# Prompt self-attention: each head group's score and value matmuls as one chained piece

## The chip, the cores and the metric

The kernel runs on one core of a Trainium2 chip. The metric is device time in microseconds from the start to the end of one execution; the median of the runs counts. PE is TensorE, DVE is VectorE, ACT is ScalarE, POOL is GpSimd, SP is SyncE, which issues the transfers. An instruction is named by the line of the kernel that made it, so L875 is line 875 of the kernel before; a line can be that of a helper.

## What is computed

One inference step of a two-layer decoder with 256 prompt tokens and 32 new tokens of eight sequences (288 columns in all). Each layer does, in short:

```python
proj = x @ w_in                                   # q, k, v of 12 heads of 64, and u, gate
q, k = rope_partial(q), rope_partial(k)
for g, (window, dilation) in enumerate(((128, 1), (512, 4), (2048, 16))):   # 4 heads each
    s = q . k[rows at distance 0, d, 2d .. window] / 8
    o[g], lse[g] = softmax(s) @ v, m + log(sum(exp(s - m)))
att = softmax(lse, over g) * o
sgu = u * (tril(w_spatial) @ layer_norm(gate) + b_spatial)
x = layer_norm(alpha * x + concat(att, sgu) @ w_mix_out)
x = layer_norm(alpha * x + cross_attention(x, memory) @ w_xo)
x = layer_norm(alpha * x + relu(x @ w_up) ** 2 @ w_down)
```

The prompt attends to itself; each new token attends to the cached keys and values of its own sequence (three caches a layer) and to the new rows.

## The kernel before

Activations lie with channels on the partitions and the 288 tokens in the free direction. A projection (`linear`, `mm3`) goes over output tiles of 128 channels; each tile is 8 input chunks with three matmuls each (L361 wh x H, L362 wh x L, L363 wl x H), since weights and activations are split into a high and a low part. ACT makes the high part wh of a weight tile (L343), DVE the low part wl (L344).

Attention is done beside the projections. A planner (`Tasks`) holds background generators with a priority; `tasks.run` draws from them as the main projection goes on, and `tasks.drain` empties them. After that a scheduler puts the instructions of each engine in their final order by priority and readiness; what stands inside `tc.high_priority()` is taken ahead of others. A dependency of kind NoSync fixes the order of two instructions on one engine without a semaphore. `burst` (L308) uses both: all its matmuls are urgent and chained. Before, only the cross-attention of the new tokens calls it.

The parts that the change and the prediction touch:

- `prompt_scores(p)` (L864), for p = 0 and 1 and three groups g: two heads (h2 = 0 and 1) in the upper and lower 64 partitions. Each head has a 256-wide score matmul (L875) and a 128-wide one (L879), f32, into a tile `tr` of its own. DVE adds the mask and takes the maximum (L883), then the softmax (L889 to L902); three transposes a group and head (L906, L908) turn the probabilities into `pt`.
- `prompt_pv(p)` (L916): for each g a 256-wide (L925) and a 128-wide (L928) value matmul for each of the two heads into one tile `acc`, which ACT and DVE copy out to attH and attL.
- `decode_scores` (L949): scores of the new tokens against the caches. GpSimd and DVE multiply cache tiles `cu` by the query (L1034 on DVE), DVE reduces them (L1035) and spreads the sums into `zs` (L1041); PE's L1047 turns zs into scores. L974 scores the new keys.
- `decode_pv` (L1090): L1101 multiplies cache value tiles `cu` with the probabilities `z`, four matmuls for each cache tile; o_1287 and o_1288 are two accumulators of layer 0, and the four tiles of o_1288 are the last ones. L1111 adds the new rows, L1122 transposes the result.
- `rope` writes the rotated q and k (L699, GpSimd among others); L777, L793 and L1014 transpose them and the values. `sgu` has L845 and L850.
- `cu` tiles are five buffers of one stream, loaded by SP in a fixed order (L148); a transfer is issued when a buffer is released by its last reader.
- The output projection starts with L361 on attH.

PSUM has three pools: `acc` with 3 tiles, `tr` with 3, `dec` with 2.

Of the kernel before, what the change touches and what calls it, by code (L numbers as in the profile page):

```python
# [1 line left out]

# [1 line left out]

# [224 lines left out]
def build(ctx, tc, I, O, worder, corder, recording):  # L229
    nc = tc.nc  # L230
    V, S, G, T = nc.vector, nc.scalar, nc.gpsimd, nc.tensor
# [23 lines left out]
    def acc(name="acc"):  # L255
        return pp.tile([128, 512], F32, name=name, tag="acc", bufs=3)
# [48 lines left out]
            tc.add_manual_dep(ins.ins, gates[name].ins.name, dep, reason="behind")  # L305
        return ins

    def burst(calls):  # L308

        last = None  # L310
        with tc.high_priority():
            for out, lhsT, rhs, start, stop in calls:
                m = T.matmul(out, lhsT, rhs, start=start, stop=stop, skip_group_check=True)
                if last is not None and not recording:
                    dep = mybir.DependencyInfo(mybir.DependencyClass.NoSync, mybir.DependencyReason.DATA)
                    tc.add_manual_dep(m.ins, last.ins.name, dep, reason="burst")
                last = m

    class Weights:
        pos = 0  # L320
# [383 lines left out]
    def layer(l, xH, xL, norm):  # L704
        tasks.flags.clear()
        flag = tasks.flag
        qT = slot([128, 6, TOK], name="qT")
        kT = slot([128, 6, TOK], name="kT")
        vn = slot([128, 2304], name="vn")
# [154 lines left out]
        def prompt_scores(p):  # L864
            pt = slot([128, 2, 3, 384], name="pt")
# [4 lines left out]
                ms.append(small(12, "m"))  # L870
            for g in range(3):
                b = [tr(), tr()]
                for h2 in range(2):
                    r = slice(64 * h2, 64 * h2 + 64)
                    T.matmul(b[h2][:, 0:256], qT[r, 2 * g + p, 128:256], kT[r, 2 * g + p, 0:256],  # L875
                             start=True, stop=True)
                for h2 in range(2):
                    r = slice(64 * h2, 64 * h2 + 64)
                    T.matmul(b[h2][:, 256:384], qT[r, 2 * g + p, 0:128], kT[r, 2 * g + p, 0:128],  # L879
                             start=True, stop=True)  # L880
                for h2 in range(2):
                    for i, (k0, k1, c) in enumerate(((0, 256, 0), (256, 384, 128))):
                        V.tensor_tensor_reduce(out=sc[h2][:, g, k0:k1], in0=b[h2][:, k0:k1], in1=mq[:, g, c:256],  # L883
                                               scale=1.0, scalar=-3e38, op0=ALU.add, op1=ALU.max,
                                               accum_out=ms[h2][:, 3 * i + g:3 * i + g + 1])
                yield 700, 1500
# [29 lines left out]
        def prompt_pv(p):  # L916
            H, L, pt = att["H"], att["L"], att.pop(f"pt{p}")
            for g in range(3):
                ps = acc()
                for tt in range(2):  # L920
                    for h2 in range(2):
                        c = 256 * g + 64 * (2 * p + h2)
                        o = ps[64 * h2:64 * h2 + 64]
                        if tt == 0:
                            T.matmul(o[:, 0:256], vn[:, c:c + 64], pt[:, h2, g, 0:256],  # L925
                                     start=True, stop=False, skip_group_check=True)
                        else:
                            T.matmul(o[:, 128:256], vn[:, 768 + c:768 + c + 64], pt[:, h2, g, 256:384],  # L928
                                     start=False, stop=True, skip_group_check=True)
                S.activation(H[:, 2 * g + p, 0:256], ps[:, 0:256], AF.Copy)  # L930
                V.tensor_sub(L[:, 2 * g + p, 0:256], ps[:, 0:256], H[:, 2 * g + p, 0:256].bitcast(F32))
                yield 650, 0
# [547 lines left out]
```

## Time and profile before

| | |
|---|---|
| median of 3 runs | 1077.78 us (1076.4 to 1078.43) |
| profiled execution | 1072.3 us |
| its span | 1070.6 us, mean granted TensorE clock 0.982 |
| PE busy | 1025.8 us, 96% of the span, 8038 matmul records |
| DVE busy | 769.4 us, 72% |
| ACT busy | 531.7 us, 50% |
| POOL busy | 191.4 us, 18% |

How to read it: PE is nearly always busy, so the stretches are to be looked at where it isn't. The trace's ends of matmuls are modelled; the distance from one start to the next says more of a matmul's cost than its length. An f32 matmul shows as two records, a pair of records on each half of the array for the two heads. In the profile, "[2.20 <-POOL kT L699]" behind an instruction means that its engine was idle for 2.20 us before it and that POOL's write of kT ended that. The granted clock is 1.00 at 2.4 GHz and 0.50 at 1.2 GHz.

### The profile page before, as it was taken

How to read it: one execution, taken by the hardware profiler on the slowest of the kernel's cores; microseconds unless marked ns; L12 is line 12 of the kernel's file. 1: busy time of each engine (PE TensorE's matmuls, PEld its weight loads, DVE VectorE, ACT ScalarE, POOL GpSimd, SP SyncE). 2: the span in 40 equal slices, each digit the busy share in tenths (PEclk: the TensorE clock that was granted, in tenths of full speed). 3: DMA queues.
4: the chain of work that ended last, by engine and by line, in shares of the span. 5: the costliest groups of instructions: out<-in, count | busy, mean ns of one | idle time of the engine just before them, and what ended most of it. 6: DMA issues, size and time to landing. Idle time of an engine off the chain costs nothing. (4 is left out here: it accounts for less than half of the span.)

```text
span 1070.6 us, 20130 instructions
## 1 busy us (share of the span) xinstructions
PE 1025.8 (96%) x8038; PEld 958.1 (89%) x8038; DVE 769.4 (72%) x1406; ACT 531.7 (50%) x1000; POOL 191.4 (18%) x151
## 2 busy tenths in 40 slices
PE   8999999999999999999978999999999999999995
PEld 7989689988799999999967995998888999999994
DVE  6698679855489756565998987897464996565656
ACT  4437546543458535353553374565353685354431
POOL 4593013000033000000458500220000410000000
PEclk8999999999999999999989899999999999999997
DMA  9989844777944555544436898357874465546431
GB/s 281 303 255 323 230 184 149 250 262 257 328 131 142 191 168 181 158 158 160 155 123 204 240 304 257 119 167 233 289 278 159 136 178 169 182 162 193 166 115 44
DMA packets 185533, 213.68 MB, mean 200 GB/s; under 512 B 5760, under 2 KB 175136, under 8 KB 185440
## 3 DMA queue, kind: packets, MB, share of 16 engines
q1 hardware_dynamic: 177216, 205.00, 60.1%
q10 hardware_dynamic: 8224, 7.41, 2.1%
q8 instruction: 63, 1.03, 0.4%
q14 instruction: 30, 0.25, 0.1%
HBM read 203.80 MB, written 8.59 MB: 198 GB/s over the span
## 5 line engine op out<-in xcount | busy, mean ns | idle before, releaser
L343 ACT ACTIVATE wh<-wraw 128x1024 fp32r<-128x1024 f32 (+1 forms) x237 | 249.5, 1054 | 297.1 <-PE acc L362 237.5
L344 DVE TENSOR_TENSOR wl<-wraw,wh 128x1024 fp32r<-128x1024 f32 (+1 forms) x237 | 311.0, 1315 | 100.4 <-ACT wh L343 99.4
L361 PE MATMUL acc<-xH,wh 128*128 128x288 f32 x728 | 219.4, 302 | 6.7 <-DVE fy L527 4.8
L363 PE MATMUL acc<-xH,wl 128*128 128x288 f32 x728 | 218.4, 301 | 3.1 <-DVE wl L344 3.1
L362 PE MATMUL acc<-xL,wh 128*128 128x288 f32 x728 | 219.0, 301 | 0.0
L361 PE MATMUL acc<-hH,wh 128*128 128x288 f32 x512 | 151.3, 295 | 0.0
L363 PE MATMUL acc<-hH,wl 128*128 128x288 f32 x512 | 151.0, 295 | 0.0
L362 PE MATMUL acc<-hL,wh 128*128 128x288 f32 x512 | 151.0, 295 | 0.0
L361 PEld LDWEIGHTS acc<-xH,wh 128*128 128x128 f32 x728 | 139.7, 192 | 8.0 <-issue 5.0
L363 PEld LDWEIGHTS acc<-xH,wl 128*128 128x128 f32 x728 | 139.2, 191 | 4.7 <-DVE wl L344 4.2
L362 PEld LDWEIGHTS acc<-xL,wh 128*128 128x128 f32 x728 | 139.6, 192 | 1.0 <-DVE fy L751 0.4
L545 POOL TENSOR_TENSOR s<-s,xres 128x288 f32<-128x288 f32 x15 | 20.3, 1354 | 445.8 <-DVE s L541 445.2
L362 PEld LDWEIGHTS acc<-hL,wh 128*128 128x128 f32 x512 | 96.4, 188 | 0.0
L361 PEld LDWEIGHTS acc<-hH,wh 128*128 128x128 f32 x512 | 96.3, 188 | 0.0
L363 PEld LDWEIGHTS acc<-hH,wl 128*128 128x128 f32 x512 | 96.2, 188 | 0.0
L361 PE MATMUL acc<-fH,wh 128*128 128x290 f32 x256 | 78.2, 306 | 1.9 <-DVE fy L527 1.9
L362 PE MATMUL acc<-fL,wh 128*128 128x290 f32 x256 | 76.8, 300 | 0.0
L363 PE MATMUL acc<-fH,wl 128*128 128x290 f32 x256 | 75.8, 299 | 0.6 <-DVE wl L344 0.6
L361 PEld LDWEIGHTS acc<-fH,wh 128*128 128x128 f32 x256 | 48.4, 189 | 2.6 <-PE acc L363 2.3
L362 PEld LDWEIGHTS acc<-fL,wh 128*128 128x128 f32 x256 | 48.5, 190 | 0.8 <-DVE fL L519 0.2
L363 PEld LDWEIGHTS acc<-fH,wl 128*128 128x128 f32 x256 | 48.0, 189 | 1.2 <-DVE wl L344 1.1
L1032 POOL TENSOR_TENSOR cu<-cu,qb 128x1024 f32<-128x1024 f32 x15 | 43.0, 2886 | 9.9 <-DMA qb<-qd 9.5
(320 smaller groups left out, 2184.5 us busy)
## 6 DMA issues: line engine op xcount, KB each, us to landing
cu<-cache_mem_kv SPq DMA_DIRECT2D x64, 512.0 KB, 7.2
wraw<-w_up SPq DMA_DIRECT2D x32, 1024.0 KB, 5.5
wraw<-w_down SPq DMA_DIRECT2D x32, 1024.0 KB, 4.8
wraw<-w_in SPq DMA_DIRECT2D x21, 1024.0 KB, 6.5
cu<-cache_kv_w SPq DMA_DIRECT2D x42, 512.0 KB, 7.2
wraw<-w_xkv SPq DMA_DIRECT2D x16, 1024.0 KB, 6.3
wraw<-w_mix_out SPq DMA_DIRECT2D x8, 1024.0 KB, 10.3
wraw<-w_xq SPq DMA_DIRECT2D x8, 1024.0 KB, 4.8
```

What stands on the lines that cost most here:

```text
L343: S.activation(h[:, r], raw[:, r], AF.Copy)
L344: gates[f"split{k}"] = behind(V.tensor_sub(lo[:, r], raw[:, r], h[:, r].bitcast(F32)), "dve")
L361: m = T.matmul(ps, wh[:, k], H[:, k], start=first, stop=False)
L362: T.matmul(ps, wh[:, k], L[:, k], start=False, stop=False)
L363: T.matmul(ps, wl[:, k], H[:, k], start=False, stop=last)
L545: eng.tensor_add(self.s, self.s, xres[:, n])
L1032: G.tensor_mul(cu, cu, qb[g])
```

## The change

`burst` gets a second argument. With `urgent=False` its first matmul keeps its ordinary priority; the others are urgent and chained behind it as before. `prompt_scores` and `prompt_pv` now collect the four matmuls of a group and queue them with `burst(calls, False)`: first both heads' 256-wide matmuls (h2 = 1, then 0), then both 128-wide ones. Before, none of these was urgent or chained, and h2 = 0 came first. No matmul, copy or transfer is added or taken away, and every operand is the same. In the kernel after, these matmuls carry line L313 (in `burst`), and lines behind `prompt_scores` move up by one (L906 is L905).

```diff
--- before.py
+++ after.py
@@ -1,4 +1,4 @@
-from contextlib import ExitStack
+from contextlib import ExitStack, nullcontext
 
 import numpy as np
 
@@ -305,16 +305,16 @@
             tc.add_manual_dep(ins.ins, gates[name].ins.name, dep, reason="behind")
         return ins
 
-    def burst(calls):
+    def burst(calls, urgent=True):
 
         last = None
-        with tc.high_priority():
-            for out, lhsT, rhs, start, stop in calls:
+        for out, lhsT, rhs, start, stop in calls:
+            with tc.high_priority() if last is not None or urgent else nullcontext():
                 m = T.matmul(out, lhsT, rhs, start=start, stop=stop, skip_group_check=True)
-                if last is not None and not recording:
-                    dep = mybir.DependencyInfo(mybir.DependencyClass.NoSync, mybir.DependencyReason.DATA)
-                    tc.add_manual_dep(m.ins, last.ins.name, dep, reason="burst")
-                last = m
+            if last is not None and not recording:
+                dep = mybir.DependencyInfo(mybir.DependencyClass.NoSync, mybir.DependencyReason.DATA)
+                tc.add_manual_dep(m.ins, last.ins.name, dep, reason="burst")
+            last = m
 
     class Weights:
         pos = 0
@@ -870,14 +870,13 @@
                 ms.append(small(12, "m"))
             for g in range(3):
                 b = [tr(), tr()]
-                for h2 in range(2):
-                    r = slice(64 * h2, 64 * h2 + 64)
-                    T.matmul(b[h2][:, 0:256], qT[r, 2 * g + p, 128:256], kT[r, 2 * g + p, 0:256],
-                             start=True, stop=True)
-                for h2 in range(2):
-                    r = slice(64 * h2, 64 * h2 + 64)
-                    T.matmul(b[h2][:, 256:384], qT[r, 2 * g + p, 0:128], kT[r, 2 * g + p, 0:128],
-                             start=True, stop=True)
+                calls = []
+                for q, c, d in (((128, 256), (0, 256), (0, 256)), ((0, 128), (0, 128), (256, 384))):
+                    for h2 in (1, 0):
+                        r = slice(64 * h2, 64 * h2 + 64)
+                        calls.append((b[h2][:, d[0]:d[1]], qT[r, 2 * g + p, q[0]:q[1]], kT[r, 2 * g + p, c[0]:c[1]],
+                                      True, True))
+                burst(calls, False)
                 for h2 in range(2):
                     for i, (k0, k1, c) in enumerate(((0, 256, 0), (256, 384, 128))):
                         V.tensor_tensor_reduce(out=sc[h2][:, g, k0:k1], in0=b[h2][:, k0:k1], in1=mq[:, g, c:256],
@@ -917,16 +916,17 @@
             H, L, pt = att["H"], att["L"], att.pop(f"pt{p}")
             for g in range(3):
                 ps = acc()
+                calls = []
                 for tt in range(2):
-                    for h2 in range(2):
+                    for h2 in (1, 0):
                         c = 256 * g + 64 * (2 * p + h2)
                         o = ps[64 * h2:64 * h2 + 64]
                         if tt == 0:
-                            T.matmul(o[:, 0:256], vn[:, c:c + 64], pt[:, h2, g, 0:256],
-                                     start=True, stop=False, skip_group_check=True)
+                            calls.append((o[:, 0:256], vn[:, c:c + 64], pt[:, h2, g, 0:256], True, False))
                         else:
-                            T.matmul(o[:, 128:256], vn[:, 768 + c:768 + c + 64], pt[:, h2, g, 256:384],
-                                     start=False, stop=True, skip_group_check=True)
+                            calls.append((o[:, 128:256], vn[:, 768 + c:768 + c + 64], pt[:, h2, g, 256:384],
+                                          False, True))
+                burst(calls, False)
                 S.activation(H[:, 2 * g + p, 0:256], ps[:, 0:256], AF.Copy)
                 V.tensor_sub(L[:, 2 * g + p, 0:256], ps[:, 0:256], H[:, 2 * g + p, 0:256].bitcast(F32))
                 yield 650, 0
```

Two places in PE's order, in which the scheduler put the work differently. In these rows "x2" stands for two matmuls alike, and a name in brackets is the engine or queue whose semaphore is waited for.

PE at the end of attention of layer 0, before: o_1288 takes the last four cache tiles (z, L1101), tr takes probability transposes (p, L906 and L908), acc takes value products (pt, L925).

```order
L1101 MATMUL o_1288<-cu,z_90 32x256 [waits DMAHW1_49,DMAHW0_49]
L906 MATMUL tr<-const,p_1210 128x128 [waits Activation_49]
L908 MATMUL tr<-const,p_1210 128x128 x2
L906 MATMUL tr<-const,p_1210 128x128 [waits Activation_49]
L908 MATMUL tr<-const,p_1210 128x128 x2
L1101 MATMUL o_1288<-cu,z_90 32x256 x3
L1101 MATMUL o_1288<-cu,z_90 32x256 [waits DMAHW3_49,DMAHW2_49]
L1101 MATMUL o_1288<-cu,z_90 32x256 x3
L1111 MATMUL o_1287<-vn,pn 128x256 x2
L925 MATMUL acc<-pt,vn 64x256 [waits Activation_49]
L925 MATMUL acc<-pt,vn 64x256 [waits DVE_49,Activation_49]
L1101 MATMUL o_1288<-cu,z_90 32x256 [waits DMAHW5_49,DMAHW4_49]
```

The same place after:

```order
L1101 MATMUL o_1288<-cu,z_90 32x256 [waits DMAHW1_49,DMAHW0_49]
L1101 MATMUL o_1288<-cu,z_90 32x256 x3
L817 MATMUL tr<-const,misc 32x128 [waits DVE_49]
L817 MATMUL tr<-const,misc 32x128
L1101 MATMUL o_1288<-cu,z_90 32x256 [waits DMAHW3_49,DMAHW2_49]
L1101 MATMUL o_1288<-cu,z_90 32x256 x3
L1101 MATMUL o_1288<-cu,z_90 32x256 [waits DMAHW5_49,DMAHW4_49]
L1101 MATMUL o_1288<-cu,z_90 32x256 x3
L1101 MATMUL o_1288<-cu,z_90 32x256 [waits DMAHW7_49,DMAHW6_49]
L1101 MATMUL o_1288<-cu,z_90 32x256 x3
L1111 MATMUL o_1288<-vn,pn 128x256
L905 MATMUL tr<-const,p_1210 128x128 [waits DVE_49]
```

The four tiles of o_1288 now follow each other, with only the two L817 between; the probability transposes that stood between them stand behind the last one, and the value products, which come as whole groups (L313), behind those.

PE in layer 1's input projection, before: two heads' scores (L875, L879), then the first matmuls of the next projection tile, then L1047 (scores from zs).

```order
L363 MATMUL acc<-xH,wl 128x288
L875 MATMUL tr<-kT,qT 128x256 [waits Activation_49]
L879 MATMUL tr<-kT,qT 128x128
L875 MATMUL tr<-kT,qT 128x256 [waits Activation_49]
L879 MATMUL tr<-kT,qT 128x128
L361 MATMUL acc<-xH,wh 128x288 [waits Activation_49]
L362 MATMUL acc<-xL,wh 128x288
L363 MATMUL acc<-xH,wl 128x288 [waits DVE_49]
L361 MATMUL acc<-xH,wh 128x288
...
L361 MATMUL acc<-xH,wh 128x288
L1047 MATMUL s_6436<-const,zs 128x16 [waits DVE_49]
L1047 MATMUL s_6436<-const,zs 128x16 x7
```

The same place after:

```order
L363 MATMUL acc<-xH,wl 128x288
L793 MATMUL tr<-const,kT 32x128 [waits Activation_49]
L793 MATMUL tr<-const,kT 32x128
L1047 MATMUL s_6436<-const,zs 128x16 [waits DVE_49]
L1047 MATMUL s_6436<-const,zs 128x16 x7
L313 MATMUL tr<-kT,qT 128x256 [waits Activation_49]
L361 MATMUL acc<-xH,wh 128x288 [waits Activation_49]
L362 MATMUL acc<-xL,wh 128x288
L363 MATMUL acc<-xH,wl 128x288
```

L1047 now stands ahead of the score matmul and of the whole next projection tile, which stood in front of it before; of the score group only the first matmul (L313) stands here.

## Rows read from the trace of the kernel before

**Rows 1.** Busy by stretch: length, PE, PEld, DVE, ACT, POOL, PEclk, DMA share, GB/s

```profile
76.10:79.60 3.50, 3.50 (x17) 3.50 (x17) 3.50 (x8) 1.06 (x1) 3.50 (x2) 0.51 1.09 348
111.70:137.30 25.60, 25.60 (x242) 14.92 (x241) 17.93 (x71) 13.42 (x41) 0.00 (x0) 1.00 0.85 245
589.20:595.00 5.80, 5.79 (x26) 5.63 (x27) 5.80 (x8) 0.81 (x2) 5.64 (x5) 0.50 0.66 207
616.00:640.00 24.00, 24.00 (x183) 23.02 (x182) 20.38 (x51) 19.46 (x44) 0.00 (x0) 1.00 0.96 314
```

**Rows 2.** PE in order of time (start, length, what, idle): two waits

```profile
75.76 0.33 PE L777 MATMUL tr<-const,kT 128*128 128x128 f32 x1 [2.20 <-POOL kT L699]
...
589.21 0.40 PE L1014 MATMUL tr<-const,qT 128*32 128x128 f32 x1 [3.03 <-POOL qT L699]
```

**Rows 3.** PE in order of time: ends of attention, layers 0 and 1

```profile
130.40 0.33 PE L906 MATMUL tr<-const,p 128*128 128x128 f32 x1
...
131.53 0.65 PE L925 MATMUL acc<-pt,vn 128*64 128x256 f32 x2
132.11 0.64 PE L1101 MATMUL o<-cu,z 128*32 128x256 f32 x8
...
137.30 0.64 PE L361 MATMUL acc<-attH,wh 128*128 128x288 f32 x3
...
659.63 0.64 PE L1101 MATMUL o<-cu,z 128*32 128x256 f32 x8
...
665.07 0.66 PE L361 MATMUL acc<-attH,wh 128*128 128x288 f32 x3
```

**Rows 4.** PE in order of time: score pieces, a pair of heads and one

```profile
63.80 0.71 PE L875 MATMUL tr<-kT,qT 64*128 64x256 f32 x4
64.34 0.40 PE L879 MATMUL tr<-kT,qT 64*128 64x128 f32 x4
64.67 0.40 PE L363 MATMUL acc<-xH,wl 128*128 128x288 f32 x1
...
65.36 0.70 PE L875 MATMUL tr<-kT,qT 64*128 64x256 f32 x2
...
66.20 0.40 PE L361 MATMUL acc<-xH,wh 128*128 128x288 f32 x1
```

**Rows 5.** PE in order of time: a whole and a torn value product

```profile
112.54 0.65 PE L925 MATMUL acc<-pt,vn 128*64 128x256 f32 x4
113.02 0.39 PE L928 MATMUL acc<-pt,vn 128*64 128x128 f32 x4
113.34 0.70 PE L875 MATMUL tr<-kT,qT 64*128 64x256 f32 x2
...
128.82 1.08 PE L925 MATMUL acc<-pt,vn 128*64 128x256 f32 x4
129.83 0.64 PE L1101 MATMUL o<-cu,z 128*32 128x256 f32 x8
```

**Rows 6.** SyncE's queue in order of time: the last value tile's issue

```profile
126.54 0.61 SPq L148 DMA_DIRECT2D cu<-cache_kv_w  x1
```

**Rows 7.** DMA issues from 126.5 to 127.1: us to landing at the end

```profile
cu<-cache_kv_w SPq DMA_DIRECT2D x1, 256.0 KB, 5.4
```

**Rows 8.** SyncE's waits from 104 to 135: total us, times, longest

```profile
SPq L148 <- PE o L1101: 14.1, 6, 6.5
```

**Rows 9.** PE in order of time: layer 1, ahead of the masked sums

```profile
609.99 0.71 PE L875 MATMUL tr<-kT,qT 64*128 64x256 f32 x4
...
611.83 0.40 PE L363 MATMUL acc<-xH,wl 128*128 128x288 f32 x1 [0.44 <-DVE wl L344]
...
613.38 1.85 PE L1047 MATMUL s<-const,zs 128*128 128x16 f32 x16
```

**Rows 10.** DVE in order of time: layer 1, the chain to zs

```profile
605.27 3.17 DVE L1034 TENSOR_TENSOR cu<-cu,qb 128x1024 f32<-128x1024 f32 x1 [0.60 <-DMA qb<-qd]
...
611.70 1.21 DVE L1041 TENSOR_TENSOR zs<-st,const 128x1024 f32<-128x1024 f32 x1
```

## Prediction

> **What bounds the kernel now.** I read the busy shares by stretch first. TensorE is the engine to follow: through the decode-value stretch of layer 0 (111.7 to 137.3) and the second half of layer 1's input projection (616 to 640) it is busy for the whole time [rows 1]. What stands in front of TensorE's queue and waits there is therefore lost one for one, and work taken off it is won one for one, unless the stage ends on a transfer. Then I looked at the places where TensorE does stop. There are two kinds. One is a wait for an operand inside the projections: 2.20 us for a rotated key at 75.76, 3.03 us for a rotated query at 589.21 [rows 2]. Behind each, the granted clock is about half for some us: 0.51 from 76.1 to 79.6, 0.50 from 589.2 to 595.0 [rows 1], that is 1.2 instead of 2.4 GHz. The other kind is the end of attention: the last of the four value tiles is used at 132.11 in layer 0 and 659.63 in layer 1, and the first matmul of the output projection starts at 137.30 and 665.07, 5.19 and 5.44 us later [rows 3]. The profiled execution (1072.3) is 0.5% below the median of the runs (1077.78). I form the sum as a difference in that execution and add it to the median; for a term of some 10 us the 0.5% does not count.
>
> **The change, part by part.** No instruction is added or removed, so the whole effect is order.
>
> *Scores.* In the trace a joined pair of heads takes 0.87 us (63.80 to 64.67), and one head alone 0.84 (65.36 to 66.20) [rows 4]. The four 256-wide pieces of the pair all start before the first 128-wide one, though the program queued them head by head: the heads run side by side, and the second costs almost nothing. The 256-wide part takes 0.54 for one head or two. Before, 24 heads stand as 5 pairs and 14 single heads: 5 x 0.87 + 14 x 0.84 = 16.1 us. In the new order one group of four stays whole and eleven are cut behind their first matmul, since only the other three are urgent: 0.87 + 11 x 0.54 + 11 x 0.87 = 16.4 us. The stretches go from 19 to 21. Entering or leaving one costs about 0.1 each (the neighbours start 0.22 to 0.24 apart there; plain projection matmuls 0.13), so +0.4. Together **+0.7** (bounds -0.5 to +2). The row speaks against a larger gain from the new order of heads. The Trainium skill (TensorE: Matmul & The Clock Gate, Part 3: Packing small matmuls) says that matmuls are strictly first in, first out. By it the second 256-wide piece would start only with the first head's 128-wide one, the old pair would cost 0.54 + 0.54 + 0.33 = 1.4 us, the new order would save 0.5 at each of the five places, and the sum below would be 2.7 smaller; the row of 0.87 disagrees with that rule.
>
> *Value products.* A whole group takes 0.80 us (112.54 to 113.34); where it stands apart, the 256-wide half alone takes 1.01 for four records of it (128.82 to 129.83) [rows 5]. About seven of twelve groups were torn; making them whole takes 0.5 us (layer 0, first half) and 1.2 us (second half of each layer) off TensorE, some 3 us. Most of it lies inside the two stage ends and is counted there, not here.
>
> *Input projection, layer 0.* The wait of 2.20 us [rows 2] has 24 matmuls between the last score piece and itself; in the new order the same transpose stands 14 matmuls further back. At 0.13 each that covers 1.8 us of the wait, and the half clock behind it might go as well (17 matmuls in 3.50 us at 0.51 [rows 1], against 2.3 at 0.13). But the next key transpose, which GpSimd feeds too, now stands 9 projection matmuls behind the first, not 18, and takes part of the wait back. I take **-1** (bounds -2.5 to +0.5).
>
> *End of attention, layer 0.* Before, the four value groups, each waiting for its cache tile, are mixed with 18 probability transposes, and three torn value-product pieces. In the new order they stand in a row, and all 18 transposes and the three whole groups stand behind the last. Three trios take 1.13 us (130.40 to 131.53) [rows 3], six 2.26. The work behind the last tile was 5.19, and in it half of the 256-wide and all 128-wide products of the three groups: 3 x (0.48 / 2 + 0.32) = 1.7 by the parts of a whole group [rows 5]. Now it holds the six trios and three whole groups: 5.19 + 2.26 + 2.40 - 1.7 = 8.15, +3.0 if the last tile comes when it came. It comes off a ring: its transfer was issued at 126.54 [rows 6] and took 5.4 to land [rows 7], 131.9, just before its use. Transfers wait for the release of an older buffer, six times and 14.1 us on this engine's groups [rows 8]. With the transposes gone from ahead, TensorE releases buffers a little earlier, at most by the 2.3 us they took. Against this, TensorE now stands idle between tiles where transposes had run, and what follows on a wait of 2 us is the half clock [rows 2]. I set the two against each other at about 1 us each and take **+3** (bounds -1 to +5.5).
>
> *Input projection, layer 1.* This is the term I trust most. The masked-score sums of the decode queries (L1047) wait for VectorE's zs. Before, they stand behind a pair of score heads and 13 matmuls of the next projection tile: TensorE goes through these from 609.99, with one wait of 0.44 for wl, and starts L1047 at 613.38 without a wait [rows 9]. VectorE begins zs at 611.70, 1.21 long [rows 10], so it is there at 612.9. In the new order L1047 stands right behind the finished tile, ahead of the lone score piece and that whole next tile. TensorE arrives at 610.0 and waits until 612.9, 2.9 us; the old 0.44 goes: +2.45. VectorE's chain starts on a transfer (605.27, after 0.60 us idle for qb [rows 10]), so a lighter VectorE doesn't bring zs forward much. Behind it TensorE had no slack up to 640 [rows 1], so it is lost for good. A wait of 2.9 lies between the 2.20 and the 3.03 that were followed by half clock: 1.2 lost behind the first, by the working above, and behind the second 26 matmuls in 5.80 us [rows 1] instead of 3.4, so 2.4. I take 2. Together **+4.4** (bounds: the wait halved and no clock loss +1; both in full +5).
>
> *End of attention, layer 1.* As in layer 0, milder: nine transposes (1.13) move behind the last value tile, and the same half of the 256-wide products (0.7): 5.44 [rows 3] becomes 7.3, +1.8. Rounded up for the waits between tiles that nothing fills any more: **+2** (bounds -1 to +5).
>
> Sum: 0.7 - 1 + 3 + 4.4 + 2 = **+9.1**, 1077.8 + 9.1 = **1086.9 us**, 0.8% slower. All terms at their friendly ends give -4.0, at their bad ends +18.
>
> **The rivals.** *Covered waits, faster.* If zs is there when TensorE comes to L1047 (it has to come 3 us earlier, or TensorE 3 us later, by a different drift of the two engines up to there), and if the tiles of the ring land earlier by what TensorE releases earlier, so that both tails are bounded by TensorE's work, what is left is 3 us of value products and 1 us in layer 0: 1077.8 - 4 + 0.7 = 1074.5. For it: TensorE is full in those stretches [rows 1], so fewer torn groups count. Against: zs hangs on a transfer and nothing in the change moves that. The point at which it decides is the wait ahead of L1047: under 0.5 us it wins. I give it 0.16.
>
> *Nothing in sum.* The ring ends both stages at its own pace (SyncE waits 14.1 us there [rows 8]) and the work moved behind the last tile is balanced by its earlier landing and the 3 us; L1047's wait of 2.5 without a clock loss is offset by layer 0's gain of 2: 1077.8 + 0.5 = 1078. I give it 0.10.
>
> *More half clock.* Behind each new wait (two between value tiles, one at L1047, one at the end of layer 1) the clock falls as behind the two waits of over 2 us [rows 2], at 1.2 to 2.4 each beyond what the sum has: three more times 2 is +6, 1093. For it: both waits of over 2 us that I read were followed by it. Against: a wait of 0.44 and work at once behind it was not. 0.22.
>
> *The change doesn't do what it says.* In part this is so already: eleven of twelve score groups are cut behind their first matmul. If the pieces, once cut, cost more than the rows show [rows 4], it is +2 on the forecast, 1089, within its range.
>
> **How the numbers follow.** Forecast (1081 to 1090) 0.52; more half clock (1090 to 1098) 0.22; nothing in sum 0.10; faster 0.16. A difference of 0.2%, 2.2 us, is about what a measurement of this kernel can tell from no change. Faster by more than that 0.16; within 0.10; slower 0.74. The range leaves out one in ten at each side: from 1075.3, within the faster case, to 1095.
>
> **What the profile after will show.** Right: TensorE idle for 2 to 3 us with VectorE's zs as releaser ahead of L1047 in layer 1, near 610, and the clock near 0.5 behind it; the first L361 on attH 7 to 8 us behind the last value tile in both layers; value groups of 0.80; no wait over 1 us near 75. Wrong: no idle time ahead of L1047; the last value tiles used over 2 us earlier against the start of their layer; score pairs that now take 0.5 us less than before. What would make it wrong in size is the clock: if no new wait is followed by a fall, 3 to 4 us of the sum are gone and 1083 is left.

## The result and the profile after

The kernel after takes 1100.35 us (median of 5 runs, 1099.47 to 1103.91) against 1077.85 (5 runs): ratio 1.0224, 95% interval 1.0207 to 1.0241. It is 22.5 us slower, 2.2%. The direction was forecast, the size was not: 9.1 was predicted and the range ended at 1095. The profiled execution has a span of 1100.4 us against 1070.6, and a mean granted clock of 0.962 against 0.982. The two profiled executions are 29.8 us apart, 7.3 more than the medians, since that of before is a short one and that of after one of the longer ones. The places below and their sizes are read from these two executions and add up to the 29.8; what the change costs in all is the 22.5 of the runs.

The instructions are the same, so the n-th projection matmul (L361) of one trace can be set against the n-th of the other. How far after is behind at each place:

| place | before, us | after, us | behind |
|---|---|---|---|
| first projection matmul | 15.98 | 15.09 | -0.9 |
| late in layer 0's input projection | 108.30 | 109.61 | +1.3 |
| first matmul of layer 0's output projection | 137.30 | 150.30 | +13.0 |
| layer 1, ahead of the masked sums | 606.90 | 619.18 | +12.3 |
| layer 1, second projection tile behind them | 615.82 | 633.68 | +17.9 |
| first matmul of layer 1's output projection | 665.07 | 694.10 | +29.0 |

Most of the loss is made at three places, each of which the prediction named: the end of layer 0's attention, the masked sums of layer 1, and layer 1's end. TensorE at the end of layer 0's attention, after (rows in order of time; the counterpart is [rows 3]):

```profile
118.02 1.07 PE L1101 MATMUL o<-cu,z 128*32 128x256 f32 x16
...
129.60 1.01 PE L1101 MATMUL o<-cu,z 128*32 128x256 f32 x8 [0.65 <-DMA cu<-cache_kv_w]
...
131.94 1.08 PE L1101 MATMUL o<-cu,z 128*32 128x256 f32 x8 [0.80 <-DMA cu<-cache_kv_w]
134.37 1.08 PE L1101 MATMUL o<-cu,z 128*32 128x256 f32 x8 [1.34 <-DMA cu<-cache_kv_w]
136.98 1.08 PE L1101 MATMUL o<-cu,z 128*32 128x256 f32 x8 [1.54 <-DMA cu<-cache_kv_w]
...
139.15 0.47 PE L905 MATMUL tr<-const,p 128*128 128x128 f32 x1
...
143.18 2.25 PE L313 MATMUL acc<-pt,vn 128*64 128x256 f32 x24
...
149.03 0.41 PE L1122 MATMUL tr<-const,od 128*128 128x128 f32 x2 [1.49 <-DVE od L1115]
150.30 1.09 PE L361 MATMUL acc<-attH,wh 128*128 128x288 f32 x3 [0.86 <-ACT attH L859]
```

The first decode value product is at 118.02; before, it was at 114.19:

```profile
114.19 1.07 PE L1101 MATMUL o<-cu,z 128*32 128x256 f32 x16
```

After, the four last cache tiles are waited for, 0.65 to 1.54 us each, the last one is used at 136.98 (132.11 before), and from there to the output projection it takes 13.3 us instead of 5.19. A transpose trio that took 0.38 in the mean [rows 3] takes 0.67 (six from 139.15 to 143.18). The same stretch by clock (columns as in [rows 1]):

```profile
112.00:129.60 17.60, 15.18 (x150) 8.95 (x149) 11.08 (x51) 9.49 (x27) 0.00 (x0) 1.00 0.75 189
129.60:143.20 13.60, 9.93 (x56) 5.20 (x56) 3.97 (x15) 3.19 (x11) 0.00 (x0) 0.51 1.01 294
143.20:150.30 7.10, 4.75 (x55) 3.34 (x54) 4.88 (x20) 2.37 (x7) 0.00 (x0) 0.98 0.34 109
```

TensorE is at half clock, 1.2 GHz, from the waits on to 143. In layer 1's input projection (the counterpart of [rows 9]):

```profile
621.96 0.38 PE L793 MATMUL tr<-const,kT 128*32 128x128 f32 x2
625.24 3.60 PE L1047 MATMUL s<-const,zs 128*128 128x16 f32 x16 [2.90 <-DVE zs L1041]
628.76 1.22 PE L313 MATMUL tr<-kT,qT 64*128 64x256 f32 x2
629.91 0.61 PE L361 MATMUL acc<-xH,wh 128*128 128x288 f32 x1
...
635.03 0.29 PE L361 MATMUL acc<-xH,wh 128*128 128x288 f32 x1
```

The masked sums (L1047) wait 2.90 us for zs, as forecast, and run at half clock, 3.5 us instead of 1.7 (before, from 613.38 [rows 9] to 615.08, the row below); what follows up to 635 runs at half clock too.

```profile
615.08 0.63 PE L777 MATMUL tr<-const,vt 128*128 128x128 f32 x4
```

VectorE's chain to zs (the counterpart of [rows 10]):

```profile
617.14 1.22 DVE L1034 TENSOR_TENSOR cu<-cu,qb 128x1024 f32<-128x1024 f32 x1 [0.45 <-DMA qb<-qd]
...
620.65 1.22 DVE L1035 TENSOR_REDUCE st<-cu 128x16 f32<-128x1024 f32 x1 [1.97 <-POOL cu L1032]
621.79 2.26 DVE L344 TENSOR_TENSOR wl<-wraw,wh 128x1024 fp32r<-128x1024 f32 x1
623.97 1.21 DVE L1041 TENSOR_TENSOR zs<-st,const 128x1024 f32<-128x1024 f32 x1
```

### The profile page after: what moved, and what is told of

The parts are those of the page before. It is cut to its first block, busy times and chain, and to the rows that moved or that the text cites. A ratio compares the mean times of both kernels' runs of the same rounds, so it can differ in the third digit from the quotient of the medians.

```text
span 1100.4 us, 20121 instructions
## 1 busy us (share of the span) xinstructions
PE 1040.5 (95%) x8038; PEld 969.6 (88%) x8038; DVE 770.2 (70%) x1406; ACT 530.5 (48%) x1000; POOL 191.4 (17%) x151
## 5 line engine op out<-in xcount | busy, mean ns | idle before, releaser
L344 DVE TENSOR_TENSOR wl<-wraw,wh 128x1024 fp32r<-128x1024 f32 (+1 forms) x237 | 314.7, 1331 | 100.9 <-ACT wh L343 99.2
L361 PE MATMUL acc<-xH,wh 128*128 128x288 f32 x728 | 220.6, 304 | 6.7 <-DVE fy L527 4.8
L363 PE MATMUL acc<-xH,wl 128*128 128x288 f32 x728 | 220.1, 303 | 1.2 <-DVE wl L344 1.2
L361 PE MATMUL acc<-hH,wh 128*128 128x288 f32 x512 | 151.3, 296 | 0.0
L363 PE MATMUL acc<-hH,wl 128*128 128x288 f32 x512 | 151.1, 295 | 0.0
L361 PEld LDWEIGHTS acc<-xH,wh 128*128 128x128 f32 x728 | 141.1, 194 | 8.7 <-issue 5.4
L363 PEld LDWEIGHTS acc<-xH,wl 128*128 128x128 f32 x728 | 140.7, 194 | 3.1 <-DVE wl L344 2.2
L361 PEld LDWEIGHTS acc<-hH,wh 128*128 128x128 f32 x512 | 96.3, 188 | 0.0
L363 PEld LDWEIGHTS acc<-hH,wl 128*128 128x128 f32 x512 | 96.3, 188 | 0.0
L361 PE MATMUL acc<-fH,wh 128*128 128x290 f32 x256 | 78.2, 306 | 1.9 <-DVE fy L527 1.9
L363 PE MATMUL acc<-fH,wl 128*128 128x290 f32 x256 | 75.8, 299 | 0.6 <-DVE wl L344 0.6
L361 PEld LDWEIGHTS acc<-fH,wh 128*128 128x128 f32 x256 | 48.3, 189 | 2.6 <-PE acc L363 2.3
L363 PEld LDWEIGHTS acc<-fH,wl 128*128 128x128 f32 x256 | 48.0, 188 | 1.3 <-DVE wl L344 1.1
L1032 POOL TENSOR_TENSOR cu<-cu,qb 128x1024 f32<-128x1024 f32 x15 | 43.1, 2890 | 8.5 <-DMA cu<-cache_kv_w 6.9
```

What stands on the lines that cost most here:

```text
L344: gates[f"split{k}"] = behind(V.tensor_sub(lo[:, r], raw[:, r], h[:, r].bitcast(F32)), "dve")
L361: m = T.matmul(ps, wh[:, k], H[:, k], start=first, stop=False)
L363: T.matmul(ps, wl[:, k], H[:, k], start=False, stop=last)
L1032: G.tensor_mul(cu, cu, qb[g])
```

## The experiments

All ratios are against the kernel before, run beside the others on the same chip. Medians of different experiments are therefore compared by these ratios.

**Which part costs.** First the two halves of the change apart. In *pv_only* the scores are queued as before:

```diff
-                burst(calls, False)              # prompt_scores
+                T.matmul(b[h2][:, 0:256], ...)   # per head, as before
```

> Value products chained as in the change, scores as before. In PE's order the masked sums of layer 1 (L1047 before) stand behind the pair of heads and 13 matmuls as before, and the transposes still stand between the last four value tiles of both layers. Theory (the order that the scores' chains bring is what costs: masked sums too early, cache ring late, transposes behind the last tile): 2 to 3 us faster than before, about 1075, no wait for zs. Rival (the value groups, whole and ahead of the decode values, hold up the cache ring): slower by over 10 us, 1088 or more.

Measured 1073.68 (12 runs), ratio 0.999, interval 0.9965 to 1.0014. In *scores_only* only the scores are chained:

```diff
-                burst(calls, False)              # prompt_pv
+                T.matmul(o[:, 0:256], vn[:, c:c + 64], pt[:, h2, g, 0:256], ...)
```

> Scores chained as in the change, value products as before. Theory: all of the loss, 1095 to 1103, with a wait of 2 to 3 us for zs in layer 1, and the first decode value product of layer 0 3 to 4 us later than before. Rival (value groups): at most half of the loss, below 1090.

Measured 1101.12, ratio 1.025 (1.0201 to 1.0299); the wait for zs is 3.1 us, and layer 0's first decode value product is 2.4 us later than before. The whole loss comes with the change of the scores. The value chains alone cannot be told from no change: they bring 3.8 us at most, by the interval, and cost 1.5 at most. The 2 to 3 us that were expected of them lie within that, but do not show.

**Which layer.** The change under a condition on the layer, the old code otherwise:

```diff
+                if l == 0:          # l1_only: l == 1
                     burst(calls, False)
+                else:               # as before
```

> The change in layer 0 alone, layer 1 as before. Theory: what the profiles show at the end of layer 0's attention, +11 to +15 of profiled time, 1088 to 1093; layer 1 gives nothing back and adds nothing. Rival (the loss in layer 1 is carried over from a late start): 1095 or more.

Measured 1088.67, ratio 1.0123 (1.0078 to 1.0168).

> The change in layer 1 alone, layer 0 as before. Theory: +6 to +8 at the masked sums and +6 to +9 at the end of attention, less some 2 us that the projections before it gained: 1088 to 1093, and this and the run with layer 0 alone add up to the whole loss. Rival (layer 1's loss needs layer 0's): below 1083.

Measured 1086.0, ratio 1.0101 (1.006 to 1.0142), 2 us below the range expected. The two add up all the same: 1.23% and 1.01%, each known to some 0.4, against 2.24% for both. Each layer loses on its own account. In layer 1 alone the wait at the masked sums was not the expected one. TensorE's waits there (us in total, times, longest):

```profile
PE s L1069 <- DVE zs L1063: 7.2, 1, 7.2
PE acc L363 <- DVE wl L344: 2.4, 1, 2.4
PE o L1123 <- DMA cu<-cache_kv_w: 2.1, 3, 1.1
```

The wait of the masked sums (L1069 in this file, L1047 in the change) for zs is 7.2 us, not 2.9. Set against the first projection matmul of the layer, TensorE comes to the masked sums as early as in the kernel after, some 62 us behind it; it is zs that comes 3.7 us later. GpSimd's product of a cache tile, which is on the way to it, starts 3.8 us later by the same measure; it waited 7.92 us for its transfer here and 6.08 in the kernel after (columns: start, duration, line and operation, in brackets the wait ahead and its releaser; first the run with layer 1 alone, then the kernel after):

```profile
605.69 5.69 POOL L1054 TENSOR_TENSOR cu<-cu,qb 128x1024 f32<-128x1024 f32 x2 [7.92 <-DMA cu<-cache_kv_w]
```

```profile
617.18 5.78 POOL L1032 TENSOR_TENSOR cu<-cu,qb 128x1024 f32<-128x1024 f32 x2 [6.08 <-DMA cu<-cache_kv_w]
```

In the six runs that have L1047 right behind the finished tile and leave zs where it was, the wait was 2.9 (after), 3.1 (*scores_only*), 5.2 (*urgent*), 5.8 (*old_heads*), 6.1 (*fill_l0*) and 7.2 us. The wait comes with the order; its size varies from run to run, and in the one pair compared here it went with the transfer.

**The heads' order or the chains.** *swap_only* is the kernel before with the loop over the heads turned round, nothing chained; *old_heads* is the change with the old loop:

```diff
-                for h2 in range(2):
+                for h2 in (1, 0):       # old_heads: the reverse
```

> Nothing chained, nothing urgent: the kernel before with the heads queued in the order 1, 0. PE's order has layer 1's masked sums behind the score pair as before, but layer 0's end like the kernel after (all first value groups and six transposes ahead of the first decode value product, the last four tiles together with two trios behind). Theory (order, not chains, is what costs): no wait over 1 us at the masked sums, +5 to +10 in layer 0, 1081 to 1087. Rival (chained and urgent pieces cost by themselves): within 2 us of before.

Measured 1084.84 (10 runs), ratio 1.0084 (1.0052 to 1.0116).

> The change with the heads in the old order 0, 1. PE's order has the masked sums of layer 1 ahead of the score piece as in the kernel after, layer 0's end with nine transposes between the last tiles and nine behind, and layer 1's end with six between and twelve behind. Theory: a wait of 2 to 7 us for zs in layer 1 and both ends longer by 4 to 8 us; 1090 to 1100. Rival (the swapped heads are the cause): within 4 us of before.

Measured 1103.71, ratio 1.0265 (1.0211 to 1.0319), 4 us more than the upper end expected. Both theories of a single cause fall. Chains without the swapped heads lose as much as the change; swapped heads without any chain lose more than a third of it (0.84% of 2.24%). What the slow kernels share is that the scheduler puts the work around the scores elsewhere. In swap_only TensorE does not wait for zs, and layer 0's end is long:

```profile
PE o L1101 <- DMA cu<-cache_kv_w: 3.7, 3, 1.5
```

```profile
114.92 1.07 PE L1101 MATMUL o<-cu,z 128*32 128x256 f32 x16
...
133.53 0.64 PE L1101 MATMUL o<-cu,z 128*32 128x256 f32 x8
...
141.58 0.66 PE L361 MATMUL acc<-attH,wh 128*128 128x288 f32 x3 [0.42 <-ACT attH L859]
```

In old_heads there are 5.8 us of waiting at the masked sums, and both ends are long: 14.2 and 14.8 us from the last tile to the output projection.

**The lone first matmul.** *urgent* puts the first matmul of each group under high priority as well:

```diff
-                burst(calls, False)
+                burst(calls)
```

> As the change, but the first matmul of each group is urgent too. The masked sums stand where they do in the kernel after, layer 0's end is as there, and layer 1's end becomes like layer 0's. Theory (order at the three places): 1098 to 1108. Rival (groups cut behind their first matmul are the cost): below 1090.

Measured 1100.88, ratio 1.0238 (1.0206 to 1.027): the priority of the first matmul is not what costs. Whether the cut costs, this run does not say. Its trace has eleven of the twelve score groups cut behind their first matmul, just as the kernel after has; so the cut does not come from the first matmul's lower priority, as the prediction had it, and what makes it is not known. What it costs by itself is small, by the rows further down; what it moves is untested.

**The clock at the end of layer 0.** *fill_l0* gives TensorE idle matmuls where it waits for the last tiles. With them the sums of the new tokens' values in layer 0 come out wrong; all the kernel's own work is there.

```diff
+                        fill = l == 0 and t == 0 and (g, i) >= (1, 7)
+                        for _ in range((4 if g == 1 else 3) if fill else 0):
+                            f = T.matmul(o2[:, 256:512], zn[:, 0], zn..., start=True, stop=True)
+                            # kept behind the last value product, ahead of the next
                         m = T.matmul(dst[32 * t:32 * t + 32], z[:, c:c + 32], mv, ...)
```

> The kernel after, with idle matmuls (zeros into an unused half of the accumulator, about 0.43 us each at full clock) queued ahead of the last five cache value tiles of layer 0: four ahead of the first of them, three ahead of each other. They fill the waits for the tiles; nine of the 18 transposes also come to stand ahead of the last tile. Theory (the waits between the tiles bring the half clock, and that makes the rest of layer 0's tail long): the clock stays at 1.00, the last tile is used within 1 us of the time in the kernel after, and the 13.3 us from there to the output projection become 7 to 8.5; 1094 to 1096. Rival (the tail is long by its work alone): 11 us or more there, 1098 or more.

Measured 1093.8, ratio 1.0177 (1.0131 to 1.0223). By the ratios that is some 5 us below the kernel after (1.0207 to 1.0241), with intervals that overlap a little: the runs alone do not quite show a gain.

```profile
132.00 1.56 PE L1104 MATMUL o<-zn 128*128 128x256 f32 x6
...
137.34 0.64 PE L1110 MATMUL o<-cu,z 128*32 128x256 f32 x8
...
144.53 0.38 PE L361 MATMUL acc<-attH,wh 128*128 128x288 f32 x1
```

```profile
112.00:129.60 17.60, 17.50 (x162) 10.61 (x164) 11.52 (x52) 9.44 (x29) 0.00 (x0) 1.00 0.75 187
129.60:143.20 13.60, 13.54 (x112) 8.92 (x106) 6.25 (x22) 4.60 (x14) 0.00 (x0) 1.00 1.05 323
```

The last tile is used when it was (137.34, after 136.98), the clock stays at 1.00, and 7.2 us follow instead of 13.3. About 1.1 of these 6.1 is three trios that the scheduler now puts ahead of the last tile. Another 2.4 are the waits for od (1.49) and attH (0.86) in the rows of the kernel after, which are gone; the scheduler also put the products of L845 and L850 elsewhere, and no run tells whether that or the clock took the waits away. The rest, some 2.7, is clock. With TensorE busy all the way the last tile came no earlier: the waits between the tiles are set by the ring. What they cost shows in the work behind them, 2.7 us of it by the clock. The gain at this place is not the gain of the kernel: in this trace the wait at layer 1's masked sums is 6.1 us instead of 2.9, which takes about 3 of it back, and layer 1's end is 4 us shorter, for which see the end of the next section.

**The masked sums.** *fill_zs* does the same in front of L1047 in layer 1 with six idle matmuls.

```diff
                 yield 0, 1500
+                for _ in range(6 if l and g == 1 else 0):
+                    f = T.matmul(s2[:, 256:512], zn[:, 0], zn..., start=True, stop=True)
+                    # kept behind the last L793 of the keys
                 for j in range(n):
```

> The kernel after, with six idle matmuls (about 2.6 us at full clock) in layer 1 in front of the masked sums, where TensorE waits 2.9 us for zs. Theory: the wait stays (zs doesn't come earlier), the half clock behind it goes, which was worth some 4.5 us (masked sums 3.5 instead of 1.7, a score piece 1.15 instead of 0.6, 20 matmuls at 0.24 instead of 0.13); 1095 to 1097. Rival (the clock falls for another reason): 1099 or more.

Measured 1099.42, ratio 1.0243 (1.0183 to 1.0303): no gain, and no answer either. TensorE came to the place 6.1 us ahead of zs in this run. The six matmuls filled 2.8 of them, and behind them there was again a long wait, and the masked sums (L1054 in this file) took 2.6 us to the next matmul instead of 1.7:

```profile
621.54 2.76 PE L1046 MATMUL s<-zn 128*128 128x256 f32 x12
627.63 2.69 PE L1054 MATMUL s<-const,zs 128*128 128x16 f32 x16 [3.33 <-DVE zs L1041]
```

*zs_first* goes at zs itself. It keeps two instructions of VectorE behind it that had stood ahead, a product that hangs on the late query transfer and a sum that hangs on GpSimd:

```diff
+                        mul = behind(V.tensor_mul(cu, cu, qb[g]), lag)
+                        if l and g == 2:
+                            behind(mul, "zs")
                     ...                          # the same for the sum
+                gates["zs"] = V.tensor_mul(z[:, 0:128 * n]..., ...)
```

> The kernel after, with one edit on VectorE in layer 1: the products and sums of the third cache group, which hang on a late query transfer and on GpSimd, may not stand ahead of zs. PE's order is that of the kernel after; the masked sums still stand ahead of the score piece and the next projection tile. Theory (the masked sums wait because zs stands behind those two on VectorE): zs is there 3 us or more earlier, the wait at the masked sums is under 0.5 us, the half clock behind it goes, 1092 to 1096. Rival (the wait is the place of the masked sums on TensorE, whatever VectorE does): a wait of 2 us or more stays, 1099 or more.

Measured 1096.6, ratio 1.0206 (1.0167 to 1.0246). The interval of the kernel after lies within this one, so the runs show no gain; the profiled execution is the shortest of four, 1092.78, and two others take over 1099. The mechanism shows in its trace:

```profile
621.52 0.40 PE L1051 MATMUL s<-const,zs 128*128 128x16 f32 x2 [0.47 <-DVE zs L1045]
...
621.98 1.63 PE L1051 MATMUL s<-const,zs 128*128 128x16 f32 x14
623.54 0.70 PE L313 MATMUL tr<-kT,qT 64*128 64x256 f32 x2
```

```profile
624.00:640.00 16.00, 16.00 (x122) 15.39 (x121) 13.41 (x32) 7.42 (x18) 0.00 (x0) 1.00 0.87 271
```

The wait is 0.47 us, the clock stays at 1.00, and the masked sums take their full-clock time. The place of the masked sums (L1051 in this file) on TensorE is that of the kernel after; so it was zs's place on VectorE that made the wait.

**Both repairs, and a kernel to beat before.** *fill_zs_first* is fill_l0 with zs_first's edit.

> Both repairs of the kernel after at once: idle matmuls ahead of the last five value tiles of layer 0 (they overwrite part of the decode values' sums there), and zs ahead of the third cache group on VectorE in layer 1. Theory (two separate losses, clock in layer 0's end and the wait at the masked sums): the gains of 6.5 and 3.7 add up, 1088 to 1092; what is left over before, 13 to 16 us, is the cache ring that starts late in both layers and the work behind the last tile. Rival (what layer 0 gains is eaten at the masked sums): 1094 or more.

Measured 1096.38, ratio 1.0195 (1.0153 to 1.0236), above the range expected: the gains do not add, as far as intervals this wide can tell. Up to the masked sums both are there: the second tile behind them is 9.3 us behind the kernel before, 17.9 in the kernel after. But the edit also moved layer 1's end, where now all 18 transposes stand behind the last tile, and from that tile to the output projection it takes 14.2 us with the clock at 0.73 in the mean, 8.7 at 1.00 in zs_first.

*pv_zs* joins the value chains, old scores and zs ahead:

> Value products chained, scores as before, and zs ahead of the third cache group on VectorE in layer 1. The wait for wl near 610 (0.4 to 3.7 us, with the half clock behind it) stood behind the same two instructions and goes: -2 to -5. But PE's order at layer 1's end becomes that of layer 0 in the kernel after up to the first decode value product (all value groups of the first half ahead of it), with 12 transposes between the last tiles: 0 to +4. In sum 1071 to 1077. Rival (the wl wait hangs on the weights' transfer): the wait stays, 1076 to 1082.

Measured 1076.02 (12 runs), ratio 1.0013 (0.9991 to 1.0035). The wait for wl did not go: TensorE still waits 2.1 us there and 1.8 us for a softmax step (L883) of VectorE just behind. No run is faster than the kernel before by more than can be measured.

## Why the prediction was right in kind and wrong in size

Right: the direction, the two mechanisms, and the place trusted most. The 2.9 us wait for zs is there, with half clock behind it; that it is there to a tenth is luck, since the same order gave 2.9 to 7.2 in six runs. The score pieces cost about what the rows said. Decode-value stretch of layer 0, after (a lone piece, a value group, the other three pieces, what follows; further down three pieces of one group with the lone first piece of the next):

```profile
112.76 0.70 PE L313 MATMUL tr<-kT,qT 64*128 64x256 f32 x2
113.39 0.87 PE L313 MATMUL acc<-pt,vn 128*64 128x256 f32 x8
114.19 0.92 PE L313 MATMUL tr<-kT,qT 64*128 64x256 f32 x6
115.04 0.44 PE L1069 MATMUL tr<-const,dp 128*128 128x128 f32 x2
...
119.87 0.93 PE L313 MATMUL tr<-kT,qT 64*128 64x256 f32 x8
120.73 0.41 PE L1101 MATMUL o<-cu,zp 128*32 128x256 f32 x2
```

A lone piece takes 0.63 with its entry (112.76 to 113.39) and the other three 0.85 (114.19 to 115.04). Where three pieces of one group and the first of the next come together they run side by side, in 0.86 (119.87 to 120.73). From the first score matmul of a stretch to the next other matmul, the 21 stretches after add up to 16.6 us, half a microsecond of it from the one at half clock at 628.76; the 19 before add up to 16.15 in the same way. The one group that stayed whole is this:

```profile
81.18 0.92 PE L313 MATMUL tr<-kT,qT 64*128 64x256 f32 x8
```

From its first record to its last start it takes 0.65 us, and the old pair at 63.80 [rows 4] takes 0.66: the new order of the heads gains nothing by itself. Of the other signs that the prediction named, the value groups of 0.80 are there (113.39 to 114.19); the ends of 7 to 8 us are not (13.3 and 12.4), and a wait of over 1 us is still there near 75 (1.6, shown further down).

Term by term, with the profiled executions:

| term | predicted | measured |
|---|---|---|
| scores' pieces | +0.7 | about +0.5 |
| input projection, layer 0 | -1 | +2.2 |
| end of attention, layer 0 | +3 | +11.7 |
| masked sums, layer 1 | +4.4 | +5.6 |
| from there to the output projection, layer 1 (predicted: the end of attention) | +2 | +11, of it +8.2 from the first decode value product on |

The scores' pieces lie within the other rows. The measured rows add up to about the difference of the profiled executions, not to the 22.5 of the runs.

**The first step that failed** is the sentence that TensorE, with the transposes gone from ahead, "releases buffers a little earlier". It was a statement on the ring that looked at its end only. The ring keeps its length whatever TensorE does in it: 17.9 us before, where TensorE is busy throughout [rows 1], and 19.0 after, with 6.1 us of waits for tiles. From the first decode value product to the last tile it takes:

| kernel, layer 0 | first product, us | last tile, us | apart |
|---|---|---|---|
| before | 114.19 | 132.11 | 17.9 |
| pv_only | 111.73 | 129.42 | 17.7 |
| swap_only | 114.92 | 133.53 | 18.6 |
| old_heads | 116.56 | 135.15 | 18.6 |
| urgent | 115.58 | 134.29 | 18.7 |
| after | 118.02 | 136.98 | 19.0 |

In both layers of all fourteen traces it is between 17.0 and 19.8. What sets the last tile, to within these 2.8 us, is thus when the ring starts, and that was not in the prediction. The run with layer 1 alone bears it out: its layer 0 is that of the kernel before, its ring starts 2.8 us earlier there (111.39), and the last tile comes 2.6 earlier (129.49). In the kernel after three whole value groups and two transpose trios stand ahead of the first decode value product, before one group and no trio, and the projection ends 1.3 later: 3.8 us in all, and the last tile is 4.9 late where I had counted on about 1 us early.

**The second** is the clock. I had set "about 1 us" against the earlier landing. From 129.6 to 143.2 the clock is 0.51. Of the 13.32 us behind the last tile TensorE is busy for 10.97; in fill_l0, at full clock, it is busy for all of 7.19. With the 1.1 us of the three trios that stand ahead of the last tile there, that makes 8.3, close to the 8.15 of the sum: the work that moves was counted rightly, and half clock adds some 2.7 us to it. The other 2.4 us of the 13.32 are the two waits for od and attH, a term that the prediction did not have. The work that had covered the waits had also kept the clock up; moved behind the last tile it is done at 1.2 GHz. The rival "More half clock" had this mechanism, but priced it at 2 us a place, by waits in the projections. At the end of attention the half clock lies over most of the work that was moved, in both layers of this trace.

**The third** is layer 0's input projection. The wait of 2.20 us was to be covered. It was split instead (the waits, TensorE, layer 0):

```profile
PE sc L974 <- POOL kT L699: 1.6, 1, 1.6
PE tr L777 <- DVE m L882: 1.6, 1, 1.6
```

Each of the two is followed by half clock; from 88 to 100 us the granted clock is 0.72. The prediction had named the next key transpose as what would take part of the gain back. It was a new-key product (L974) and a value transpose that waited for the softmax on VectorE, and they took all of it.

**Why the value chains show no gain.** Many of the torn groups lie between the start of the ring and its end, and the ring takes 17.7 us in pv_only too; over layer 0's end its trace neither gains nor loses against the kernel before. It is 4.5 us ahead up to layer 1's masked sums and 2.1 behind just after them: TensorE waits 3.66 us for wl (L363, at 610.50) and goes on at a clock of 0.54 (609 to 616.6). So part of the gain is made and lost again at one place; this is one execution, and no run took it apart. The prediction counted what they do inside the ends (whole groups, 2.40 - 1.7) and nothing beside that. The rival of covered waits counted all 3 us as a gain, and pv_only gives 1.1, with an interval that holds both 3 and none.

**Layer 1's end, and what is open.** Layer 1's ring does not start late against its projection: 3.0 us behind the last projection matmul, 4.4 before. From the last tile to the output projection it takes 12.4 us instead of 5.44. In the run with layer 1 alone, in fill_l0 and in zs_first TensorE has the same order there as in the kernel after, matmul for matmul, and takes 8.7, 9.2 and 8.7. The stretch with layer 1 alone and in the kernel after (columns as in [rows 1]):

```profile
668.52:677.25 8.73, 6.86 (x73) 4.74 (x73) 6.19 (x24) 3.38 (x10) 0.00 (x0) 1.00 0.92 365
```

```profile
681.69:694.10 12.41, 10.54 (x73) 7.06 (x74) 5.50 (x22) 3.18 (x8) 0.00 (x0) 0.68 0.58 228
```

The idle time is the same, 1.87 us; the same 73 matmul records take 6.86 us at 1.00 and 10.54 at 0.68. So of the 7.0 us by which this end grew, 3.7 are half clock and 3.3 are order, for which the prediction had 1.8. The half clock there belongs to this execution and not to the order: the waits for the last two tiles, 1.09 and 0.56 us with layer 1 alone and 1.14 and 0.69 in the kernel after, differ by little. Why the clock fell in the one and not in the other is not shown, and how often it falls in the kernel's other executions is not known. How the scheduler comes to put work where it does is not shown by any run.

## What to carry to other kernels

A change of priorities is a change of the whole order: here a chain of four score matmuls moved decode work, transposes and a sum that nobody had touched, and each repair moved something else. Before such a change, look for the pieces that a ring of buffers or another engine paces, and ask of each whether it starts later, not only whether it ends earlier. Work that covers a wait can be worth more than its own time: behind the uncovered waits of layer 0's end and of the masked sums TensorE worked at half clock (0.51 and 0.50), though behind those of layer 1's end it did so in one execution and not in another of the same order.

## What the runs showed of the hardware

One VectorE instruction has two durations. zs, 128 x 1024, takes 1.21 us in the kernel before [rows 10] and in the kernel after, but in zs_first it runs while GpSimd multiplies cache tiles (L1032), and then:

```profile
618.03 3.43 DVE L1045 TENSOR_TENSOR zs<-st,const 128x1024 f32<-128x1024 f32 x1
```

```profile
617.65 6.04 POOL L1032 TENSOR_TENSOR cu<-cu,qb 128x1024 f32<-128x1024 f32 x2 [6.57 <-DMA cu<-cache_kv_w]
```

3.43 us, not 1.21. Here L1032 had been running for 0.38 us when zs began. The product at 605.27 in [rows 10], 3.17 long, also began while L1032 was running (604.96 to 610.7):

```profile
604.96 5.73 POOL L1032 TENSOR_TENSOR cu<-cu,qb 128x1024 f32<-128x1024 f32 x2 [6.42 <-DMA qb<-qd]
```

In the kernel after the same product, at 617.14, takes 1.22, and there it was GpSimd that came second: its L1032 starts at 617.18, in the row shown with the run of layer 1 alone. So in these three cases VectorE's instruction is about three times as long when GpSimd was first, and not when VectorE was; the first of GpSimd's two products, taken singly, takes 3.43 us where it came second and 2.40 in the kernel before. The Trainium skill (SBUF — State Buffer, SBUF: two separate sides) says that the two engines share a pair of ports under an exclusive lock that is held for a whole instruction, which counts for a VectorE instruction with two inputs in SBUF, as these have, and that what comes second is blocked. The three cases agree with it; no run here took the two apart on purpose. An edit that brings zs forward can thus pay for it with a zs three times as long.
